# First-phase attention heads: operands written from PSUM into the attention's tiles, and the mLSTM's key units named first

## The chip, the cores and the metric

One core of a Trainium2 chip runs the kernel. The metric is device time in microseconds (us), of which smaller is better: a kernel is run several times and the median stands for it. A profile of one more execution shows every engine: TensorE (PE: matmuls, transposes), VectorE (DVE), ScalarE (ACT), GpSimd (POOL), SyncE (SP, which here issues nearly all DMA transfers).

## The reference

One layer of a hybrid encoder, run for 1024 frames of a new stream and 32 frames of a running one. The input is modulated, projected once, and the projection's columns go to three groups of heads: mLSTM (a matrix memory, 4 heads), FoX (attention with a forget gate, 8 heads of 64) and a gMLP gate. Their outputs are concatenated and projected, then a normalisation and a SwiGLU feed-forward follow. The attention part, cut:

```python
h = x * (1 + sc1) + sh1
mq, mk, mv, mo, mi, mf, fq, fk, fv, ff, gu, gv = jnp.split(h @ w_in, split_at, axis=-1)
...
def _fox_prompt(q, k, v, logf):
    Ft = jnp.cumsum(logf, axis=1).transpose(0, 2, 1)
...
        logits = (jnp.einsum('bthd,bshd->bhts', qi, k) * FOX_SCALE
                  + Fi[..., None] - Ft[:, :, None, :])
        logits = jnp.where(pos_k[None, :] <= pos_q[:, None], logits, -jnp.inf)
        p = jax.nn.softmax(logits, axis=-1)
        return jnp.einsum('bhts,bshd->bthd', p, v)
```

`fk` is also an output. The mLSTM needs the running sums and maxima of its gates (`li`, `lf`) before its chunks, and the forget gates of the attention come from the same small projection.

## The kernel before

All matmuls are in float32 precision by halves: each operand is split into a high half (rounded to the multiplier's format) and a low half (the rest), and a product is three matmuls (`gemm`, L112): hi x hi, hi x lo, lo x hi. The contraction over 1024 features is eight steps, so a block of 128 outputs by n frames costs 24 matmuls of n columns. Weights come in pieces of 512 KB (`raw`), ACT makes the high half (L105), DVE or POOL the low half (L106).

Frames come in two groups: group 0 is frames 0 to 511, group 1 the next 512 and the 32 of the running stream. A feature-major unit (`fm_unit`) projects 128 outputs; group 0 is cut into two pieces of 256 frames, group 1 into two of 272. Its results stand in a PSUM bank of pool "g", which has three.

For the attention a unit is one head: 64 rows of q and 64 of k. `evac_qk` (L359) takes a bank apart: ACT writes the scaled high half (`qkh`, L366), DVE the low half (`qkl`, L367), POOL their sum for the output k (`qkr`, L368). The halves are stored to the arrays `dqh` and `dql` in memory, the sum to the output. `fox` (L671) later loads a head's operands from there in eight loads and v in one: `qp` = (q hi over q lo), `k1` = (k hi twice), `q2` = (q hi, and four rows of the forget gates from `dfs`), `k2` = (k lo, and four such rows). Two matmuls per piece then give the logits S in a bank (L717 with `qp` and `k1`, L718 with `q2` and `k2`), DVE takes maxima, ACT the exponential (L726), PE transposes (L753), and so on to the output, which leaves its bank by an ACT copy (`fo`, L773) and a DVE addition (`fr`, L774).

In the first phase, `ORDER` (L42) names the units one after the other: q0 to q7 are the attention heads' projections, f0 to f7 their attention over the first 512 frames, k0 and k1 the mLSTM's keys (p: POOL makes the low halves), s the mLSTM's states, v and o token-major projections, m0 to m3 the mLSTM heads, a a piece of the late modulation (`ada`, L179 and following, which loads 512 KB into one of two buffers). The gates' code stands ahead of all of them. The text order isn't the order of execution: a list scheduler, which models the engines' times, places each engine's instructions; f and m units have high priority. Tiles come from pools with a fixed number of buffers per name, and an instruction that needs a buffer again waits for the buffer's last users. Each engine then takes its own instructions strictly in the placed order.

The attention's operand tiles stand in pool `mx0`, which is opened after the gates' pool is closed and uses its memory. The number of buffers is `foxbufs`: k1, qp and q2, k2, v, and one more.

Of the kernel before, what the change touches and what calls it, by code (L numbers as in the profile page):

```python
# [7 lines left out]
F32 = mybir.dt.float32  # L8
# [7 lines left out]
P = 128  # L16
D = 1024
KT = 8
# [20 lines left out]
MLB = (1, 2, 3, 4, 5)  # L39
RESE = "pp"  # L40
TAFF = ("aaaaaaaa", "aaaaaaav")
ORDER = "q0 f0 q1 a f1 a q2 f2 k0 k1p s a q3 f3 a v q4 f4 a q5 f5 o a m0 q6 f6 a m1 q7 m2 f7 a m3"  # L42
ADAPOS = 4
GENG = (0, 1, 1, 0)
FP = (0, 0)
# [20 lines left out]
def f(ap):  # L66
    return ap.bitcast(F32)


class Kernel:  # L70
# [10 lines left out]
    def t(self, pool, shape, dt=F32, tag=None, bufs=None):  # L81
        self.n += 1
        kw = {} if bufs is None else {"bufs": bufs}
        return pool.tile(shape, dt, tag=tag, name=f"{self.phase}_{tag}_{self.n}", **kw)
# [274 lines left out]
    def evac_qk(self, h):  # L359
        nc = self.nc  # L360

        def evac(o, n, ps):
            hi = self.t(self.sm, [P, 272], F32R, "qkh", 3)
            lo = self.t(self.sm, [P, 272], F32R, "qkl", 2)
            kr = self.t(self.sm, [P, 272], F32, "qkr", 3)
            nc.scalar.activation(hi[:, :n], ps, AF.Copy, scale=self.qsc)  # L366
            nc.vector.scalar_tensor_tensor(lo[:, :n], ps, self.qsc, f(hi[:, :n]), ALU.mult, ALU.subtract)  # L367
            nc.gpsimd.tensor_tensor(kr[:, :n], f(hi[:, :n]), f(lo[:, :n]), ALU.add)  # L368
            self.store(self.dqh[h, :, o:o + n], f(hi[:, :n]))
            self.store(self.dql[h, :, o:o + n], f(lo[:, :n]))  # L370
            self.store(self.d["o_kT"][h, :, o:o + n], kr[64:, :n])
            if o + n == T:
                nc.gpsimd.tensor_copy(self.qks[:, h, :], kr[:, n - NS:n])
        return evac

    def evac_mqk(self, i, scale):
        nc = self.nc

        def evac(o, n, ps):
            r = self.t(self.sm, [P, 272], F32, "qkr", 3)  # L380
            nc.scalar.activation(r[:, :n], ps, AF.Copy, scale=scale)
            self.store(self.dmqk[:, i, o:o + n], r[:, :n])
        return evac
# [288 lines left out]
    def fox(self, h, chunks):  # L672
        self.phase = "fox"
        mx = self.mx
        q0, q1 = chunks[0][0] * P, (chunks[-1][-1] + 1) * P
        nq, nk, nb = q1 - q0, q1, q1 // P
        t = lambda shape, dt, tag, bufs: self.t(mx, shape, dt, tag, bufs)
        b = self.foxbufs
        k1 = t([P, nk], F32R, "k1", b[0])
        qp = t([P, nq], F32R, "qp", b[1])  # L680
        k2 = t([68, nk], F32R, "k2", b[2])
        q2 = t([68, nq], F32R, "q2", b[1])
        v = t([P, nb, P], F32R, "v", b[3])
        qs = slice(q0, q1)
        self.load(f(qp[0:64]), self.dqh[h, 0:64, qs])
        self.load(f(qp[64:128]), self.dql[h, 0:64, qs])
        self.load(f(k1[0:64]), self.dqh[h, 64:128, :nk])
        self.load(f(k1[64:128]), self.dqh[h, 64:128, :nk])
        self.load(f(q2[0:64]), self.dqh[h, 0:64, qs])
        self.load(f(q2[64:68]), self.dfs[h, 2:6, qs])  # L690
        self.load(f(k2[0:64]), self.dql[h, 64:128, :nk])
        self.load(f(k2[64:68]), self.dfs[h, 0:4, :nk])
        self.load(f(v), self.dv[:, :nb, h * P:(h + 1) * P])
        for tiles in chunks:
            o = tiles[0] * P - q0
            n = len(tiles) * P
            yield from self.fox_chunk(h, tiles, nk, n, k1, k2, qp[:, o:o + n], q2[:, o:o + n], v)

    def fox_chunk(self, h, tiles, W, nq, k1, k2, qp, q2, v):
        nc, mx = self.nc, self.mx  # L700
        nb = tiles[-1] + 1
        t = lambda shape, dt, tag, bufs: self.t(mx, shape, dt, tag, bufs)
        b5 = self.foxbufs[4]
        probs = []
        for i in tiles:
            n = (i + 1) * P
            qc = slice((i - tiles[0]) * P, (i - tiles[0] + 1) * P)
            half = n if n <= 512 else (n // 2 + 127) // 128 * 128
            cuts = [(0, half)] + ([(half, n)] if half < n else [])
            mxs = self.t(mx, [P, 2], F32, "fmx", 3)  # L710
            sums = self.t(mx, [P, 2], F32, "fsm", 3)
            pr = t([P, W], F32, "p", 4)
            banks = []
            for x, (lo, hi) in enumerate(cuts):
                s = self.t(self.pss, [P, 512], F32, "s")
                w = hi - lo
                nc.tensor.matmul(s[:, :w], qp[:, qc], k1[:, lo:hi], start=True, stop=False)  # L717
                nc.tensor.matmul(s[:, :w], q2[:, qc], k2[:, lo:hi], start=False, stop=True)  # L718
                if hi == n:
                    nc.vector.tensor_tensor(s[:, w - P:w], s[:, w - P:w], self.maskneg, ALU.add)  # L720
                nc.vector.tensor_reduce(mxs[:, x:x + 1], s[:, :w], AX.X, ALU.max, negate=True)
                banks.append(s)
            if len(cuts) > 1:
                nc.vector.tensor_tensor(mxs[:, 0:1], mxs[:, 0:1], mxs[:, 1:2], ALU.min)  # L724
            for x, (lo, hi) in enumerate(cuts):
                nc.scalar.activation(pr[:, lo:hi], banks[x][:, :hi - lo], AF.Exp, bias=mxs[:, 0:1],  # L726
                                     accum_out=sums[:, x:x + 1])
            if len(cuts) > 1:
                nc.vector.tensor_tensor(sums[:, 0:1], sums[:, 0:1], sums[:, 1:2], ALU.add)
            nc.vector.reciprocal(sums[:, 0:1], sums[:, 0:1])  # L730
            if FP[tiles[0] // 4]:
                nc.scalar.activation(pr[:, :n], pr[:, :n], AF.Copy, scale=sums[:, 0:1])
            else:
                nc.vector.tensor_scalar(pr[:, :n], pr[:, :n], sums[:, 0:1], None, ALU.mult)
            probs.append(pr)
            yield
            self.phase = "fox"


        o = self.t(self.po, [P, 512], F32, "o")  # L740
        full = tiles[0] + 1
        order = [0] + list(range(full, nb)) + list(range(1, full))
        units = [order[x:x + 2] for x in range(0, nb, 2)] if full > 1 else [[0], [1], [2, 3]]
        held = None
        for unit in units:
            ps = self.t(self.pt, [P, 512], F32, "t")
            at, e = [], 0
            for b in unit:
                first = max(0, b - tiles[0])
                w = nq - first * P  # L750
                for y in range(first, len(tiles)):
                    c = e + (y - first) * P
                    nc.tensor.transpose(ps[:, c:c + P], probs[y][:, b * P:(b + 1) * P], self.ident)  # L753
                at.append((b, slice(e, e + w), slice(first * P, nq)))
                e += w
            ph = t([P, 512], F32R, "pth", b5)
            pl = t([P, 512], F32R, "ptl", 2)
            nc.scalar.copy(ph[:, :e], ps[:, :e])
            nc.vector.tensor_tensor(pl[:, :e], ps[:, :e], f(ph[:, :e]), ALU.subtract)
            for b, c, q in at:  # L760
                nc.tensor.matmul(o[:, q] if b == 0 else o[0:64, q], v[:, b, :] if b == 0 else v[:, b, 0:64],
                                 pl[:, c], start=b == 0, stop=False)
                if b == 0 and full == 1:
                    held = ph
                else:
                    nc.tensor.matmul(o[:, q], v[:, b, :], ph[:, c], start=False, stop=full > 1 and b == order[-1])
            yield
            self.phase = "fox"
        if held is not None:
            nc.tensor.matmul(o[:, :nq], v[:, 0, :], held[:, :nq], start=False, stop=True)  # L770
        tmp = t([64, nq], F32, "fo", 1)
        r = t([64, nq], F32, "fr", 1)
        nc.scalar.copy(tmp[:, :nq], o[64:128, :nq])  # L773
        nc.vector.tensor_tensor(r[:, :nq], o[0:64, :nq], tmp[:, :nq], ALU.add)  # L774
        c = tiles[0] // 4
        o = tiles[0] * P - GO[c]
        self.store(self.dmix[c][64 * (h % 2):64 * (h % 2) + 64, 2 + h // 2, o:o + nq], r[:, :nq])
# [474 lines left out]
    def run(self):  # L1252
# [68 lines left out]
        more(T1[3])  # L1321
        s2 = ExitStack()
        self.mx = self.pool("mx0", ctx=s2)
        self.foxbufs = (2, 1, 1, 2, 3)

        def emit(x):
            eng = nc.gpsimd if x[-1] == "p" else nc.vector
# [4 lines left out]
            if x[0] == "m":  # L1332
                return self.mlstm(i)
            if x[0] == "q":
                self.fm_unit(w3[2 + i], self.evac_qk(i), (0, 1) if i < QD else (0,), eng)
            elif x[0] == "k":
                self.fm_unit(w3[i], self.evac_mqk(2 + i, 0.125), eng=eng)
            elif x[0] == "s":
# [256 lines left out]
```

## Time and profile before

| | us |
|---|---|
| median of the three runs | 1391.1 (1388.4 to 1398.72) |
| profiled execution, its own time | 1389.64 |
| its span in the trace | 1387.8 |

The tables of the profile are read like this. A timeline row has the start in us, the duration, the engine, the line, the operation, the output and the inputs by the program's names, the shape and the count; in brackets the idle time before it and what ended it. A row of the waits' table has the engine and line, what was waited for, the total in us, how often, and the longest. A row of the windows' table has the stretch, its length, each engine's busy time with its instruction count (PE, its weight loads, DVE, ACT, POOL), the granted PE clock, the DMA share and GB/s. A group's row has the count, the busy time in us and the mean in ns, then the idle time before it and what ended it.

### The profile page before, as it was taken

What the parts mean: (1) busy time and instruction counts of PE and PEld (TensorE: products, weight loads), DVE (VectorE), ACT (ScalarE), POOL (GpSimd) and SP (SyncE); (2) the same over time, 40 slices, a digit from 0 to 9 for tenths busy, and PEclk for the clock granted to TensorE, in tenths of its full rate; (3) what the DMA queues carried; (4) which work ended last, traced back from release to release, by engine and by line L of the source; (5) the groups of instructions that cost most, each with busy time, mean ns of one, the idle gap of its engine ahead of it and who ended that gap; (6) DMA issues with size and microseconds to landing.
All of it is one profiled execution on the core that took longest, in us unless ns stands there. A gap on an engine that the chain in (4) does not pass through costs nothing.

```text
span 1387.8 us, 25846 instructions
## 1 busy us (share of the span) xinstructions
PE 1344.1 (97%) x9651; PEld 1236.2 (89%) x9651; DVE 1030.4 (74%) x2190; ACT 641.0 (46%) x1249; POOL 260.2 (19%) x292
## 2 busy tenths in 40 slices
PE   7999999999999799999999999999999999999996
PEld 4899988899999678888887889899999999999996
DVE  5548656678788657777776766678898988888777
ACT  3313234444555344545544455345574544545355
POOL 0103200052267400000000000264610000000341
PEclk9999999999999899999999999999999999999998
DMA  9764577585765665554543442564587767453321
GB/s 361 260 217 135 165 239 213 173 252 167 234 209 152 194 182 155 141 140 118 138 117 86 112 122 81 192 176 132 159 221 200 217 163 205 145 176 113 102 90 65
DMA packets 133557, 233.09 MB, mean 168 GB/s; under 512 B 22308, under 2 KB 75180, under 8 KB 133432
## 3 DMA queue, kind: packets, MB, share of 16 engines
q1 hardware_dynamic: 128120, 221.34, 51.7%
q0 software_dynamic: 5168, 9.96, 4.7%
q8 instruction: 76, 1.25, 0.4%
q14 instruction: 49, 0.40, 0.1%
q10 hardware_dynamic: 144, 0.14, 0.0%
HBM read 197.50 MB, written 53.81 MB: 181 GB/s over the span
## 4 chain that ended last, share of the span: by engine, by line
PE 69%; DVE 4%; DMA 2%; ACT 1%; issue 1%; POOL 0%; SPq 0%; DVEq 0%; ACTq 0%
PE up_g L117 5%; PE up_g L118 5%; PE up_g L119 5%; PE dn_g L119 4%; PE dn_g L117 4%; PE dn_g L118 4%; PE sup_u L119 3%; PE sup_u L117 3%; PE sup_u L118 3%; PE wo_g L118 2%; PE wo_g L119 2%; PE wo_g L117 2%; PE sup_g L118 2%; PE sup_g L119 2%; PE sup_g L117 2%; PE fox_t L753 2%
## 5 line engine op out<-in xcount | busy, mean ns | idle before, releaser
L117 PE MATMUL up_g<-mlstm_ah,up_whi 128*128 128x512 f32 (+1 forms) x384 | 142.8, 372 | 3.6 <-DVE fm_qkl L367 2.7
L118 PE MATMUL up_g<-mlstm_al,up_whi 128*128 128x512 f32 (+1 forms) x384 | 143.0, 372 | 0.6 <-DVE mlstm_al L1008 0.6
L119 PE MATMUL up_g<-mlstm_ah,up_wlo 128*128 128x512 f32 (+1 forms) x384 | 142.4, 371 | 0.0
L284 PE MATMUL tm_g<-tm_whi,start_h1l 128*128 128x256 f32 (+1 forms) x384 | 110.0, 287 | 0.0
L282 PE MATMUL tm_g<-tm_whi,start_h1h 128*128 128x256 f32 (+1 forms) x384 | 109.6, 287 | 0.0
L283 PE MATMUL tm_g<-tm_wlo,start_h1h 128*128 128x256 f32 (+1 forms) x384 | 109.5, 286 | 0.0
L117 PE MATMUL fm_g<-start_h1h,fm_whi 128*128 128x256 f32 (+2 forms) x344 | 102.1, 302 | 6.9 <-DVE fm_qkl L367 2.7
L118 PE MATMUL fm_g<-start_h1l,fm_whi 128*128 128x256 f32 (+2 forms) x344 | 101.5, 295 | 0.2 <-DVE start_h1l L223 0.2
L119 PE MATMUL fm_g<-start_h1h,fm_wlo 128*128 128x256 f32 (+2 forms) x344 | 100.6, 294 | 0.0
L1127 ACT CAST sup_whi<-sup_raw 128x1024 fp32r<-128x1024 f32 x54 | 56.0, 1048 | 90.3 <-PE dn_u L118 46.5
L117 PEld LDWEIGHTS up_g<-mlstm_ah,up_whi 128*128 128x128 f32 x384 | 74.5, 194 | 16.2 <-DVE fm_qkl L367 2.9
L118 PEld LDWEIGHTS up_g<-mlstm_al,up_whi 128*128 128x128 f32 x384 | 74.6, 194 | 12.6 <-DVE up_actl L1061 0.8
L119 PEld LDWEIGHTS up_g<-mlstm_ah,up_wlo 128*128 128x128 f32 x384 | 74.6, 194 | 10.7
L105 ACT CAST up_whi<-up_raw 128x1024 fp32r<-128x1024 f32 x50 | 52.4, 1049 | 61.1 <-PE dn_g L118 22.5
L726 ACT ACTIVATE fox_p<-fox_s,fox_fmx 128x384 f32<-128x384 f32 (+2 forms) x96 | 55.1, 579 | 49.1 <-DVE fox_fmx L724 43.6
L117 PEld LDWEIGHTS fm_g<-start_h1h,fm_whi 128*128 128x128 f32 x344 | 65.3, 191 | 12.7 <-DVE fm_qkl L367 3.2
L982 DVE SCALAR_TENSOR_TENSOR wo_z<-dn_g,start_mod,wo_z 128x512 f32<-128x512 f32 (+4 forms) x120 | 60.3, 521 | 21.1 <-PE dn_g L119 20.5
L1128 DVE TENSOR_TENSOR sup_wlo<-sup_raw,sup_whi 128x1024 fp32r<-128x1024 f32 x54 | 68.0, 1263 | 10.4 <-ACT sup_whi L1127 10.4
L282 PEld LDWEIGHTS tm_g<-tm_whi,start_h1h 128*128 128x128 f32 x384 | 72.3, 189 | 1.9 <-issue 1.2
L284 PEld LDWEIGHTS tm_g<-tm_whi,start_h1l 128*128 128x128 f32 x384 | 72.3, 188 | 1.5 <-issue 1.2
L117 PE MATMUL dn_g<-up_acth,dn_whi 128*128 128x512 f32 (+2 forms) x200 | 73.5, 368 | 0.0
L118 PE MATMUL dn_g<-up_actl,dn_whi 128*128 128x512 f32 (+2 forms) x200 | 73.4, 368 | 0.0
(571 smaller groups left out, 4591.4 us busy)
## 6 DMA issues: line engine op xcount, KB each, us to landing
up_raw<-w_gu SPq DMA_DIRECT2D x50, 512.0 KB
dn_raw<-w_dn SPq DMA_DIRECT2D x28, 512.0 KB
ada_late<-w_ada SPq DMA_DIRECT2D x24, 512.0 KB
wo_raw<-w_o SPq DMA_DIRECT2D x24, 512.0 KB
sup_raw<-w_gu SPq DMA_DIRECT2D x20, 512.0 KB
start_dp<-w_gu SPq DMA_DIRECT2D x19, 512.0 KB
start_dp<-w_gu POOLq DMA_DIRECT2D x19, 512.0 KB, 7.7
sup_raw<-start_dp SPq DMA_DIRECT2D x18, 512.0 KB
```

Of the source, the lines that this page charges most:

```text
L105: nc.scalar.copy(hi[:, :w], raw[:, :w])
L117: nc.tensor.matmul(ps, hi, xh(k), start=start and k == 0, stop=False)
L118: nc.tensor.matmul(ps, hi, xl(k), start=False, stop=False)
L119: nc.tensor.matmul(ps, lo, xh(k), start=False, stop=stop and k == n - 1)
L282: nc.tensor.matmul(ps[:, :ncol], xh, hi, start=k == 0, stop=False)
L283: nc.tensor.matmul(ps[:, :ncol], xh, lo, start=False, stop=False)
L284: nc.tensor.matmul(ps[:, :ncol], xl, hi, start=False, stop=k == 7)
L726: nc.scalar.activation(pr[:, lo:hi], banks[x][:, :hi - lo], AF.Exp, bias=mxs[:, 0:1], accum_out=sums[:, x:x + 1])
L753: nc.tensor.transpose(ps[:, c:c + P], probs[y][:, b * P:(b + 1) * P], self.ident)
L982: self.lastz = self.nc.vector.scalar_tensor_tensor(z[:, m, x:y], ps[:, x - a:y - a], g[i], z[:, m, x:y], ALU.mult, ALU.add)
L1127: nc.scalar.copy(h, x)
L1128: tt(l, x, f(h), ALU.subtract)
```

## The change

1. `ORDER` names k0 and k1p first, then q0 f0 q1, and s stands before q2.
2. A q unit is no longer an `fm_unit` but a `head_unit`. It makes one product of 512 columns for group 0, in one bank, and writes the halves from that bank into the attention's tiles: ACT writes q hi into `qp`, DVE q lo beside it, ACT k hi into one half of `k1`, DVE k lo into `k2`, ACT k hi again into the other half of `k1` and q hi into `q2`; two ACT copies take k for the output. Only the halves of k go to `dqh` and `dql`. The four forget-gate rows of `q2` and `k2`, and v, are still loaded. Heads 0 and 1 project their group 1 as before.
3. `fox` takes a head's tiles where `head_unit` left them; the second phase loads them as before.
4. `foxbufs` is (2, 2, 2, 2, 3) for (2, 1, 1, 2, 3); `qkh` and `qkr` have two buffers for three.
5. The output's `fo` and `fr` are one tile.

```diff
-ORDER = "q0 f0 q1 a f1 a q2 f2 k0 k1p s a q3 f3 a v q4 f4 a q5 f5 o a m0 q6 f6 a m1 q7 m2 f7 a m3"
+ORDER = "k0 k1p q0 f0 q1 a f1 s a q2 f2 a q3 f3 a v q4 f4 a q5 f5 o a m0 q6 f6 a m1 q7 m2 f7 a m3"
...
-            hi = self.t(self.sm, [P, 272], F32R, "qkh", 3)
+            hi = self.t(self.sm, [P, 272], F32R, "qkh", 2)
             lo = self.t(self.sm, [P, 272], F32R, "qkl", 2)
-            kr = self.t(self.sm, [P, 272], F32, "qkr", 3)
+            kr = self.t(self.sm, [P, 272], F32, "qkr", 2)
...
+    def head_tiles(self, h, nq, nk):
+        b = self.foxbufs
+        t = lambda shape, tag, bufs: self.t(self.mx, shape, F32R, tag, bufs)
+        return (t([P, nk], "k1", b[0]), t([68, nk], "k2", b[2]), t([P, nq], "qp", b[1]), t([68, nq], "q2", b[1]),
+                t([P, nk // P, P], "v", b[3]))
+
+    def head_unit(self, h):
+
+        nc = self.nc
+        w = self.weights(self.d["w_in_f"][2 + h], KT, P)
+        self.phase = "head"
+        k1, k2, qp, q2, v = self.heads[h] = self.head_tiles(h, 512, 512)
+        self.load(f(q2[64:68]), self.dfs[h, 2:6, :512])
+        self.load(f(k2[64:68]), self.dfs[h, 0:4, :512])
+        self.load(f(v), self.dv[:, :4, h * P:(h + 1) * P])
+        ps = self.t(self.pg, [P, 512], F32, "g")
+        self.gemm(ps, w, slice(0, P), *self.h1parts(0, 512))
+        lo, hi = slice(0, 64), slice(64, 128)
+        nc.scalar.activation(qp[lo], ps[lo], AF.Copy, scale=0.125)
+        nc.vector.scalar_tensor_tensor(qp[hi], ps[lo], 0.125, f(qp[lo]), ALU.mult, ALU.subtract)
+        nc.scalar.copy(k1[hi], ps[hi])
+        nc.vector.tensor_tensor(k2[lo], ps[hi], f(k1[hi]), ALU.subtract)
+        nc.scalar.copy(k1[lo], ps[hi])
+        nc.scalar.activation(q2[lo], ps[lo], AF.Copy, scale=0.125)
+        for o in (0, 256):
+            kr = self.t(self.sm, [P, 272], F32, "qkr", 2)
+            nc.scalar.copy(kr[hi, :256], ps[hi, o:o + 256])
+            self.store(self.d["o_kT"][h, :, o:o + 256], kr[hi, :256])
+        self.store(self.dqh[h, hi, :512], f(k1[hi]))
+        self.store(self.dql[h, hi, :512], f(k2[lo]))
+        if h < QD:
+            evac = self.evac_qk(h)
+            self.phase = "fm"
+            for o, n in self.ranges((1,)):
+                ps = self.t(self.pg, [P, 512], F32, "g")
+                self.gemm(ps[:, :n], w, slice(0, P), *self.h1parts(o, n))
+                evac(o, n, ps[:, :n])
...
-            r = self.t(self.sm, [P, 272], F32, "qkr", 3)
+            r = self.t(self.sm, [P, 272], F32, "qkr", 2)
...
+        if h in self.heads:
+            k1, k2, qp, q2, v = self.heads.pop(h)
+        else:
+            k1, k2, qp, q2, v = self.head_tiles(h, nq, nk)
...
-        tmp = t([64, nq], F32, "fo", 1)
-        r = t([64, nq], F32, "fr", 1)
-        nc.scalar.copy(tmp[:, :nq], o[64:128, :nq])
-        nc.vector.tensor_tensor(r[:, :nq], o[0:64, :nq], tmp[:, :nq], ALU.add)
+        r = t([64, nq], F32, "fo", 1)
+        nc.scalar.copy(r[:, :nq], o[64:128, :nq])
+        nc.vector.tensor_tensor(r[:, :nq], o[0:64, :nq], r[:, :nq], ALU.add)
...
-        self.foxbufs = (2, 1, 1, 2, 3)
+        self.foxbufs = (2, 2, 2, 2, 3)
+        self.heads = {}
...
-                self.fm_unit(w3[2 + i], self.evac_qk(i), (0, 1) if i < QD else (0,), eng)
+                self.head_unit(i)
```

More of the change, by code (lines that the diff above doesn't have):

```diff
@@ L676, in fox @@
         nq, nk, nb = q1 - q0, q1, q1 // P
[L677 to L693, printed above, removed]
+        if h in self.heads:
+            k1, k2, qp, q2, v = self.heads.pop(h)
+        else:
+            k1, k2, qp, q2, v = self.head_tiles(h, nq, nk)
+            qs = slice(q0, q1)
+            self.load(f(qp[0:64]), self.dqh[h, 0:64, qs])
+            self.load(f(qp[64:128]), self.dql[h, 0:64, qs])
+            self.load(f(k1[0:64]), self.dqh[h, 64:128, :nk])
+            self.load(f(k1[64:128]), self.dqh[h, 64:128, :nk])
+            self.load(f(q2[0:64]), self.dqh[h, 0:64, qs])
+            self.load(f(q2[64:68]), self.dfs[h, 2:6, qs])
+            self.load(f(k2[0:64]), self.dql[h, 64:128, :nk])
+            self.load(f(k2[64:68]), self.dfs[h, 0:4, :nk])
+            self.load(f(v), self.dv[:, :nb, h * P:(h + 1) * P])
         for tiles in chunks:
```

## The prediction, made before the changed kernel was run

> **What bounds the kernel now.** I read the page's busy table and chain of waits first, then the table of waits of TensorE (PE), then the timeline at those waits, and last the windows around them.
>
> ```profile
> PE 1344.1 (97%) x9651; PEld 1236.2 (89%) x9651; DVE 1030.4 (74%) x2190; ACT 641.0 (46%) x1249; POOL 260.2 (19%) x292
> PE 69%; DVE 4%; DMA 2%; ACT 1%; issue 1%; POOL 0%; SPq 0%; DVEq 0%; ACTq 0%
> ```
>
> PE is the bound: 97% busy. ScalarE (ACT) and GpSimd (POOL) have room. A change can pay only by shortening PE's matmuls or by closing holes in PE's line. These are the holes in the part that changes:
>
> ```profile
> PE fox_s L717 <- DMA fox_qp<-start_dql: 4.3, 3, 1.7
> PE fm_g L117 <- DVE fm_qkl L367: 2.7, 1, 2.7
> ```
>
> ```profile
> 137.33 0.28 PE L119 MATMUL fm_g<-start_h1h,fm_wlo 128*128 128x256 f32 x1
> ...
> 138.04 0.28 PE L119 MATMUL fm_g<-start_h1h,fm_wlo 128*128 128x256 f32 x1
> 141.02 0.58 PE L117 MATMUL fm_g<-start_h1h,fm_whi 128*128 128x256 f32 x1 [2.70 <-DVE fm_qkl L367]
> ```
>
> ```profile
> 105.00:170.00 65.00, 62.30 (x512) 61.36 (x511) 49.32 (x120) 19.09 (x41) 19.45 (x29) 0.97 0.49 143
> 170.00:215.00 45.00, 43.27 (x348) 37.50 (x347) 24.00 (x74) 17.10 (x47) 1.46 (x2) 1.00 0.80 241
> 215.00:260.00 45.00, 42.34 (x354) 39.26 (x352) 25.59 (x65) 20.07 (x51) 3.68 (x5) 1.00 0.73 212
> ```
>
> At 141 us PE waits 2.70 us for an evacuation (fm_qkl) that stands on VectorE (DVE) in the middle of the mLSTM gates; behind it a matmul takes 0.58 us instead of 0.28, and the window's granted clock is 0.97: 3% of 65 us, so about 2.0 us more. That hole costs 4.7 us. The other three are the loads of the attention's operands:
>
> ```profile
> 202.66 0.47 PE L717 MATMUL fox_s<-fox_k,fox_qp 128*128 128x128 f32 x2 [1.73 <-DMA fox_qp<-start_dql]
> 218.20 0.47 PE L717 MATMUL fox_s<-fox_k,fox_qp 128*128 128x128 f32 x2 [1.34 <-DMA fox_qp<-start_dql]
> 255.71 0.47 PE L717 MATMUL fox_s<-fox_k,fox_qp 128*128 128x128 f32 x2 [1.20 <-DMA fox_qp<-start_dql]
> ```
>
> These are 4.27 us, and the clock of their windows stays at 1.00, so no more hangs on them.
>
> **The loads removed.** Per head the stores and reloads of qp, k1, k2 and q2 go, so the three waits above have nothing left to wait for: minus 4.3 us. What takes the load's place is a chain on ACT and DVE that reads the PSUM bank; for heads 1 to 7 the order has 40 or more PE rows (at 0.118 us, 4.7 us) between the end of a head's product and the head's first S row, so I count no new wait there in the likeliest case. SyncE (SP) issues 56 instructions fewer; the small rows of the forget gate (4 partitions of q2 and k2) and v are still loaded, long before their use.
>
> **The wider product.** A head's product is 24 matmuls of 512 columns in place of 48 of 256.
>
> ```profile
> 801.48 0.39 PE L119 MATMUL dn_g<-up_acth,dn_wlo 128*128 128x512 f32 x1
> ...
> 802.88 0.39 PE L119 MATMUL dn_g<-up_acth,dn_wlo 128*128 128x512 f32 x1
> ```
>
> Six matmuls lie between the starts in both pairs: 1.40/6 = 0.233 us for 512 columns, 0.71/6 = 0.118 us for 256. So 24 x 0.233 = 5.60 against 48 x 0.118 = 5.68: 0.08 a head, minus 0.6 us for eight. For 272 columns I scale: 0.118 x 272/256 = 0.126.
>
> **The new start of the attention.** This is the term that decides. On PE, around head 0's first S products, before (names: fm_g is a projection's PSUM bank, tm_g a token-major one, fox_s the S bank, ada_t a late modulation row):
>
> ```order
> L118 MATMUL fm_g_2511<-start_h1l_170,fm_whi_2507 128x256
> L717 MATMUL fox_s_1703<-fox_k_282_1686,fox_qp_1687 128x128
> L717 MATMUL fox_s_1714<-fox_k_282_1686,fox_qp_1687 128x256
> L119 MATMUL fm_g_2511<-start_h1h_169,fm_wlo_2508 128x256
> L117 MATMUL fm_g_2511<-start_h1h_169,fm_whi_2507 128x256
> ```
>
> and now (gates_t are the gates' transposes):
>
> ```order
> L117 MATMUL fm_g_2036<-start_h1h_171,fox_whi_1985 128x272
> L118 MATMUL fm_g_2036<-start_h1l_172,fox_whi_1985 128x272
> L119 MATMUL fm_g_2036<-start_h1h_171,fox_wlo_1986 128x272
> L185 MATMUL ada_t_1496<-start_ident_121,ada_adas_1509 128x128 x2
> L179 MATMUL ada_t_1518<-ada_late_1519,start_c_63_182 32x256 x4
> L752 MATMUL fox_s_1904<-head_k_288_1785,head_qp_1787 128x128
> L752 MATMUL fox_s_1915<-head_k_288_1785,head_qp_1787 128x256
> L753 MATMUL fox_s_1904<-head_k_289_1786,head_q_291_1788 128x128
> L753 MATMUL fox_s_1915<-head_k_289_1786,head_q_291_1788 128x256
> ```
>
> The S rows moved from PE's row 1061 to its row 928, right behind the gates, with no projection left to fill ahead of them. What they need hangs on ACT. Before, ACT's rows around the decay factor d0c (an exponential of two small rows that the gates send out and fetch back through memory):
>
> ```order
> L381 ACTIVATE fm_qkr_2413<-fm_g_2388 128x256
> L513 ACTIVATE fm_d0c_2480<-fm_d0c_2480 128x18
> L381 ACTIVATE fm_qkr_2441<-fm_g_2416 128x272
> L495 ACTIVATE start_col_178<-start_col_178 128x9x12
> L182 COPY ada_adas_1509<-ada_t_1496 128x256
> ```
>
> and now:
>
> ```order
> L366 ACTIVATE fm_qkh_1891<-fm_g_1866,start_qsc_147 128x272
> L551 ACTIVATE fox_d0c_2216<-fox_d0c_2216 128x18
> L394 ACTIVATE head_qp_1787<-head_g_1793 64x512
> L394 ACTIVATE head_qp_1991<-head_g_1997 64x512
> L533 ACTIVATE start_col_178<-start_col_178 128x9x12
> L182 COPY ada_adas_1509<-ada_t_1496 128x256
> L396 COPY head_k_288_1785<-head_g_1793 64x512
> L396 COPY head_k_334_1989<-head_g_1997 64x512
> L398 COPY head_k_288_1785<-head_g_1793 64x512
> L399 ACTIVATE head_q_291_1788<-head_g_1793 64x512
> ```
>
> The first head's evacuation now stands behind d0c, and ACT takes its rows in order. Their times, with the gates' last steps on DVE, and then the forms of 64x512 and 64x256:
>
> ```profile
> 163.79 0.22 ACT L513 ACTIVATE fm_d0c<-fm_d0c 128x18 f32<-128x18 f32 x1 [3.27 <-DMA fm_d0c<-start_dd]
> ...
> 164.43 0.28 ACT L495 ACTIVATE start_col<-start_col 128x108 f32<-128x108 f32 x1
> 165.12 0.37 ACT L182 COPY ada_adas<-ada_t 128x256 f32<-128x256 f32 x1 [0.40 <-PE ada_t L179]
> ```
>
> ```profile
> 134.33 0.28 DVE L439 TENSOR_TENSOR gates_fr<-gates_ft,gates_fr 8x128 fp32r<-8x128 f32 x1 [0.87 <-ACT gates_fr L438]
> ...
> 136.62 2.47 DVE L440 TENSOR_SCALAR gates_fr<-gates_fr 8x256 fp32r<-8x256 f32 x1
> ...
> 141.00 0.28 DVE L440 TENSOR_SCALAR gates_fr<-gates_fr 8x256 fp32r<-8x256 f32 x1
> ...
> 144.02 1.11 DVE L440 TENSOR_SCALAR gates_fr<-gates_fr 8x256 fp32r<-8x256 f32 x1
> ...
> 146.97 0.47 DVE L367 SCALAR_TENSOR_TENSOR fm_qkl<-fm_g,start_qsc,fm_qkh 128x256 fp32r<-128x256 f32 x1
> ...
> 156.40 0.15 DVE L479 TENSOR_TENSOR gates_d<-gates_m0x,gates_me 4x9 f32<-4x9 f32 x1
> 156.58 1.35 DVE L487 TENSOR_TENSOR gates_rs<-gates_rb,gates_me 4x1152 f32<-4x1152 f32 x1
> ```
>
> ```profile
> L773 ACT COPY fox_fo<-fox_o 64x256 f32<-64x256 f32 x16 | 5.9, 370 | 15.0 <-PE fox_o L766 14.8
> L773 ACT COPY fox_fo<-fox_o 64x512 f32<-64x512 f32 x8 | 4.7, 584 | 3.7 <-PE fox_o L770 3.6
> L774 DVE TENSOR_TENSOR fox_fr<-fox_o,fox_fo 64x512 f32<-64x512 f32 x8 | 5.4, 677 | 0.8 <-ACT fox_fo L773 0.8
> ```
>
> Call T the end of gates_rs, 157.9 before. On DVE the order has six evacuations (fm_qkl) between the gates' steps before, and one now:
>
> ```order
> L505 COPY gates_me_1433<-gates_cm_243_1417 4x1
> L506 TENSOR_TENSOR gates_m_244_1432<-gates_me_1433,gates_gb_1414 4x1
> L367 TENSOR_SCALAR fm_qkl_1858<-fm_g_1832,start_qsc_147,fm_qkh_1857 128x272
> L504 TENSOR_SCALAR gates_cm_243_1417<-gates_cm_242_1416,gates_m_244_1432 4x128
> L505 COPY gates_me_1433<-gates_cm_243_1417 4x1
> ```
>
> That is where this one moved: PE's second head product waits for it. Five fewer are 5 x 0.47 = 2.4 us. If the stretched steps shrink to 0.28 too, as POOL loses its work beside them, another 2.2 + 0.8 go, and the 0.87 that DVE waited for ACT. T then lies between 157.9 - 2.4 = 155.5 and 157.9 - 6.3 = 151.6; below this I allow 149, as more rows like these may shrink. I take 152, near the end where the stretch goes with its cause.
>
> d0c started 163.79 - 156.55 = 7.2 us after gates_d ended and 5.9 after T; its loads and stores are unchanged, so it ends at T + 6.1. Then ACT does two qp (2 x 0.58), col 0.28, adas 0.37 and the first k1 0.58: T + 8.5. DVE's k2 (0.68) and ACT's second k1 (0.58) follow one on the other: S can start at T + 9.7 = 161.7.
>
> PE reached row 873 at 138.2, so row 801, up to which the widths are the same, at 138.2 - 72 x 0.118 = 129.7. The first head's product (5.6) and two of 272 (6.0) end at 141.3. From there to S it has the second head's product 5.6, one of 272 at 3.0, twelve late modulation rows and eleven transposes at no more than 0.12 (2.8): 11.4. It loses 161.7 - 141.3 - 11.4 = **9.0 us** (6 for T = 149, 12.5 for 155.5) in two or three waits: for fm_qkl_1858, for the evacuation behind gates_rs, and for adas and S. A halved clock inside this stretch is hidden by it; the last wait, some 4 us, can leave 2.0 us of it behind: 0 to 2, I take 1. The next product waits for the bank that q2 (0.58) and two copies of 0.37 still read, less four S rows: 0.7.
>
> One price stands outside: ada_t_1518's load of 512 KB starts only when ada_t_1496 has read the buffer, some 6 us before S. Its nearest row is on another queue:
>
> ```profile
> start_dp<-w_gu POOLq DMA_DIRECT2D x19, 512.0 KB, 7.7
> ```
>
> At 7.7 it ends last by 1.7 us; I take 0, since this stretch moves little else (DMA share 0.49 above), and keep 1.7 for the range.
>
> [...]
>
> **Later stretches.** ACT gets four operations of 0.58 and two of 0.37 a head (3.1) for two of 0.47 (0.9): 17 us more in all, in windows where it is busy 17 to 20 us of 45. DVE gets 2 x 0.68 for 2 x 0.48, POOL gives up two additions. Beside PE this is free where work lies between. Not free is the copy of k: only two buffers are left, and an exponential stands behind a copy that waits for a store. A store's wait was seen here:
>
> ```profile
> L381 ACT ACTIVATE fm_qkr<-fm_g 128x256 f32<-128x256 f32 x4 | 1.5, 385 | 10.1 <-DMA o_kT<-fm_qkr 4.5 <-PE fm_g L119 2.5 <-issue 1.7
> ```
>
> 4.5 us over four; a head product of 5.6 us stands on PE behind the first of these, so I take 1 us, between 0 and 4.5. After about 385 us PE's order is the same as before. The merged fo/fr tile and the two extra operand buffers need no instruction.
>
> **Sum.** 9.0 + 1 + 0.7 + 1 = 11.7 added; 4.7 + 4.3 + 0.6 = 9.6 removed: +2.1. The profiled execution took 1389.6 us (span 1387.8, 1.8 around it), 1.5 under the median of the three runs. 1389.6 + 2.1 = **1392 us**. Its bounds: -9.6 + 6 + 0.7 = -2.9, so 1387, to -9.6 + 12.5 + 2 + 0.7 + 1.7 + 4.5 = +11.8, of which I keep 10, since not all are bad at once: 1399.
>
> **Rivals.**
> *A, the holes only change places:* the new waits cost what the wait at 141 did (4.7), since d0c is fetched sooner with fewer stores queued ahead on SP. For it: 56 instructions go from that queue. Against it: DMA was not busy there. 1389.6 - 4.3 - 0.6 = 1385.
>
> *B, slower:* the ACT queue at the k copies. Two buffers, and each next copy waits for a store, with the exponentials behind it. It decides from the point where PE has under 4.5 us (38 rows at 0.118) between an exponential and the transposes that read it. At four heads of eight that is 4 x 4.5 = 18 us: 1410. For it: ACT takes its rows strictly in order and gets the copies in place of POOL. Against it: ACT is half idle, and the order puts head products there.
>
> *C, wide matmuls gain more:* if a 512-column matmul followed at the pace of a 256-column one, 24 x 0.118 would go from each of eight heads: 22.7 us, 1392 - 22 = 1370. The row of 0.233 speaks against it. [...]
>
> *D, not what it says:* the S rows still wait for a load, the small rows or v, as long as they did for qp: the 4.3 stay, 1396. Against it: they are issued early.
>
> **The numbers.** Forecast 0.50, A 0.18, B 0.14, C 0.02, D 0.10, and 0.06 for what I don't see, half to each side. Two runs of this kernel can't be told apart under about 1% (14 us). Faster by that: C and half the unseen, 0.05. Slower: B, less a little where it strikes fewer heads, and half the unseen, 0.15. Within: 0.80. The forecast's own range is 1387 to 1399; with A below and smaller forms of B above, 1381 to 1404 leaves out about 2 in 10.
>
> **What would show it.** No wait of fox_s for fox_qp; d0c's exponential ending about 6 us after gates_rs, with the first qp behind it; S's first row near 162; a wait of 3 to 5 us right ahead of it; pace 0.233 in the head products. It would be wrong if S starts under 8 us after gates_rs, if T stays at 157, or if the waits after 170 us grow rather than go.

## The result and the profile after

| | median, us | ratio to before (95% interval) |
|---|---|---|
| before, 20 runs | 1390.06 | |
| changed kernel, 20 runs | 1386.86 | 0.9972 [0.9961, 0.9982] |
| changed kernel again on another chip (11 runs; before 1387.49) | 1385.75 | 0.9977 [0.9961, 0.9993] |

The change makes the kernel 3.2 us faster by the medians where 2.1 us slower had been forecast. (The ratios and their intervals are estimated from all runs; the quotients of the medians are 0.9977 and 0.9987.) First the same views as before. The waits of TensorE (PE) in the changed kernel:

```profile
PE up_g L117 <- ACT lna_tmp L1037: 3.4, 1, 3.4
PE ada_t L179 <- DMA ada_late<-w_ada: 2.8, 1, 2.8
PE fm_g L117 <- DVE fm_qkl L367: 2.4, 2, 2.0
PE mlstm_t L598 <- DVE fox_ptl L794: 2.2, 1, 2.2
...
PE fox_s L752 <- ACT fox_p L761: 1.9, 1, 1.9
```

No wait of fox_s for a load is left, and the wait of 2.7 us at 141 us is gone. New are the wait for a late modulation's load and one of the mLSTM's transposes behind the attention. Its windows:

```profile
105.00:170.00 65.00, 61.66 (x446) 56.51 (x445) 47.52 (x131) 22.56 (x50) 12.76 (x20) 0.95 0.40 121
170.00:215.00 45.00, 44.91 (x328) 38.40 (x327) 32.00 (x88) 26.01 (x67) 2.12 (x3) 1.00 0.65 199
215.00:260.00 45.00, 45.00 (x331) 40.00 (x330) 22.49 (x55) 22.52 (x52) 1.13 (x2) 1.00 0.49 158
```

From 170 to 260 us the busy time of PE shows hardly a hole (89.9 of 90 us, before 85.6). From 105 to 170 us it lost more than before: 61.66 us busy for 62.30, at a clock of 0.95 for 0.97.

The start of the attention, in the timelines of DVE, ACT and PE:

```profile
149.92 1.35 DVE L525 TENSOR_TENSOR gates_rs<-gates_rb,gates_me 4x1152 f32<-4x1152 f32 x1
```

```profile
156.05 0.22 ACT L551 ACTIVATE fox_d0c<-fox_d0c 128x18 f32<-128x18 f32 x1 [8.51 <-DMA fox_d0c<-start_dd]
156.17 1.05 ACT L394 ACTIVATE head_qp<-head_g 64x512 fp32r<-64x512 f32 x2
...
159.19 0.58 ACT L398 CAST head_k<-head_g 64x512 fp32r<-64x512 f32 x1 [0.44 <-DVE head_k L397]
```

```profile
157.72 0.44 PE L185 MATMUL ada_t<-start_ident,ada_adas 128*128 128x128 f32 x2 [0.15 <-ACT ada_adas L182]
160.97 1.08 PE L179 MATMUL ada_t<-ada_late,start_c 128*32 128x256 f32 x8 [2.81 <-DMA ada_late<-w_ada]
161.98 0.80 PE L752 MATMUL fox_s<-head_k,head_qp 128*128 128x128 f32 x2
```

The gates end at T = 151.3 (152 was taken), and S starts at 162.0 (161.7). But the reason is another one: the evacuation is done at 159.8, T + 8.5, and PE stands for 2.8 us before the load of 512 KB. That load was the price put at 0, with 1.7 us kept for the range.

### The profile page after: what moved, and what is told of

The parts are those of the page before. It is cut to its first block, busy times and chain, and to the rows that moved or that the text cites. A ratio compares the mean times of both kernels' runs of the same rounds, so it can differ in the third digit from the quotient of the medians.

```text
span 1384.6 us, 25402 instructions
## 1 busy us (share of the span) xinstructions
PE 1343.1 (97%) x9459; PEld 1226.1 (89%) x9459; DVE 1031.2 (74%) x2190; ACT 655.5 (47%) x1281; POOL 244.8 (18%) x276
## 4 chain that ended last, share of the span: by engine, by line
PE 83%; DVE 9%; DMA 4%; ACT 2%; issue 2%; POOL 1%; SPq 0%; DVEq 0%; ACTq 0%; POOLq 0%
PE up_g L117 5%; PE up_g L118 5%; PE up_g L119 5%; PE dn_g L119 4%; PE dn_g L117 4%; PE dn_g L118 4%; PE tm_g L282 3%; PE tm_g L283 3%; PE tm_g L284 3%; PE sup_u L119 3%; PE sup_u L117 3%; PE sup_u L118 3%; PE wo_g L118 2%; PE wo_g L119 2%; PE wo_g L117 2%; PE fox_t L788 2%
## 5 line engine op out<-in xcount | busy, mean ns | idle before, releaser
L119 PEld LDWEIGHTS up_g<-mlstm_ah,up_wlo 128*128 128x128 f32 x384 | 73.2, 191 | 10.6
L106 DVE TENSOR_TENSOR up_wlo<-up_raw,up_whi 128x1024 fp32r<-128x1024 f32 x50 | 66.8, 1336 | 14.0 <-ACT up_whi L105 13.3
L283 PEld LDWEIGHTS tm_g<-tm_wlo,start_h1h 128*128 128x128 f32 x384 | 72.3, 188 | 2.3 <-issue 2.1
L119 PE MATMUL dn_g<-up_acth,dn_wlo 128*128 128x512 f32 (+2 forms) x200 | 73.3, 366 | 0.0
L117 PE MATMUL fm_g<-start_h1h,fm_whi 128*128 128x272 f32 (+2 forms) x200 | 60.6, 312 | 5.9 <-DVE fm_qkl L367 2.0
```

The source lines that it names most:

```text
L106: (eng or nc.vector).tensor_tensor(lo[:, :w], raw[:, :w], f(hi[:, :w]), ALU.subtract)
L117: nc.tensor.matmul(ps, hi, xh(k), start=start and k == 0, stop=False)
L119: nc.tensor.matmul(ps, lo, xh(k), start=False, stop=stop and k == n - 1)
L283: nc.tensor.matmul(ps[:, :ncol], xh, lo, start=False, stop=False)
```

## The experiments

Single executions of one kernel differ by several us (28 runs of the kernel before on one chip lie between 1383.8 and 1392.1), so three profiles of each kernel were compared by stage (the repeated profiles below supply the others). For every matmul I took the time to the next matmul's start, less the usual distance for its width (the median over the run); the sum over a stage is PE's loss there. The part of it that falls on half clock (stretches in which the granted clock is 0.50) comes from the granted clock in windows of 1 us. Means of three profiles, us:

| stage, us | before: waits + half clock | after: waits + half clock | difference |
|---|---|---|---|
| 0 to 105 (unchanged) | 20.1 + 0 | 20.3 + 0 | +0.2 |
| 105 to 170, gates, start of attention | 3.8 + 1.7 | 5.5 + 3.4 | +3.4 |
| 170 to 260, heads 0 to 3 | 15.3 + 0.6 | 8.3 + 0 | -7.6 |
| 260 to 345, mLSTM and heads | 8.5 + 0 | 10.6 + 0 | +2.1 |
| 345 to 400 | 4.9 + 0 | 5.9 + 2.3 | +3.3 |
| 400 to 480, order unchanged | 10.8 + 5.4 | 9.9 + 2.3 | -4.0 |
| 480 to 1365, order unchanged | 29.6 + 2.0 | 28.3 + 1.7 | -1.6 |

The sum is -4.2; with the 0.6 us of the wider product it is -4.8, and the mean spans (1388.5 and 1383.8) differ by 4.7. The half clock is 9.7 us in all in both: it moved, and as a whole it neither gave nor took. The timed runs agree: on the second chip their granted clock is 0.991 on the mean, before and after. The 4.7 us are more than the 3.2 of the medians, and two of the three profiles of before took 2.8 and 4.0 us more than the median of their chip (1389.35 for 1386.53, 1392.09 for 1388.12).

Where the difference is made shows at the first row from which PE's order is the same to the end in both kernels (6677 matmuls), first before, then after:

```profile
386.19 0.28 PE L118 MATMUL wo_g<-mlstm_al,wo_whi 128*128 128x256 f32 x1
```

```profile
389.39 0.47 PE L118 MATMUL wo_g<-mlstm_al,wo_whi 128*128 128x256 f32 x1
```

In the other profiles it starts at 389.5 and 390.7 us before, at 389.9 and 389.6 after. The changed kernel thus comes there no sooner, 0.8 us later on the mean. What is left takes 1001.6, 998.1 and 999.5 us before and 995.2, 994.0 and 993.3 after. By the table, waits fell by 2.2 us and half clock rose by 3.4 between 105 and 400 us; behind 400 us waits fell by 2.2 and half clock by 3.4. So in these profiles what the removed loads give is given back inside the changed part, and the difference lies behind it, in instructions that the change leaves as they were.

**The two parts of the change, each alone.** The new ORDER in the kernel before:

```diff
-ORDER = "q0 f0 q1 a f1 a q2 f2 k0 k1p s a q3 f3 ..."
+ORDER = "k0 k1p q0 f0 q1 a f1 s a q2 f2 a q3 f3 ..."
```

> The kernel before with the new ORDER alone (keys first), operands still through memory. If the gain is the removed loads: no gain here, 0 to +3 us, since the loads' waits (4.3 us) stay. If the gain comes from the gates ending earlier with no evacuations between them: -2 to -4 us, and the wait of 2.7 us at 138 us is gone.

Measured: 1.0006 [0.9990, 1.0022]. The two waits as its waits' table has them:

```profile
PE fox_s L717 <- DMA fox_qp<-start_dql: 3.4, 2, 2.1
PE gates_t L492 <- DVE gates_rs L487: 2.0, 1, 2.0
```

The order alone gives nothing: the loads' waits stay, and the wait for an evacuation among the gates is replaced by one of 2.0 us for the gates themselves. The other half, the changed kernel with the old ORDER:

> The changed kernel with the old ORDER: operands straight from PSUM, keys after head 2. If the gain is the removed loads: -3 to -5 us; the first S no longer stands behind the decay factor, so the stall of 3 us ahead of it should be smaller. If the order is what pays: 0 to +2 us.

Measured: 1412.84 us against 1386.53, 1.0194 [1.0169, 1.0219], 26 us slower. Both expectations fall. Its timeline of PE, its waits and the window:

```profile
130.87 0.29 PE L119 MATMUL fm_g<-start_h1h,fox_wlo 128*128 128x272 f32 x1
154.73 2.15 PE L530 MATMUL gates_t<-start_ident,gates_rs 128*128 128x128 f32 x9 [23.57 <-DVE gates_rs L525]
```

```profile
154.61 1.07 ACT L394 ACTIVATE head_qp<-head_g 64x512 fp32r<-64x512 f32 x2 [14.11 <-DVE gates_rs L525]
```

```profile
105.00:170.00 65.00, 37.56 (x231) 31.83 (x230) 43.20 (x126) 16.19 (x38) 7.69 (x18) 0.74 0.29 83
```

PE stands still for 23.6 us until the gates end. The heads' first evacuation (head_qp) waits for the same instruction, since the operand tiles lie in the gates' memory, so the two heads' banks, two of three, stay full (ACT then empties both, x2). The third is full as well: the product of 272 columns that ends before the wait is copied out only at 167.8 us, because its copy needs a buffer that POOL frees late, after the first head's stores of k.

```profile
167.00 1.48 POOL L368 TENSOR_TENSOR fm_qkr<-fm_qkh,fm_qkl 128x272 f32<-128x272 f32 x2 [21.41 <-DMA o_kT<-head_qkr]
```

```profile
167.79 0.49 ACT L366 ACTIVATE fm_qkh<-fm_g,start_qsc 128x272 fp32r<-128x272 f32 x1 [2.65 <-POOL fm_qkr L368]
```

The two buffers of qkh and qkr may thus have a share in this stall; the old ORDER with three was not run. With loads, the heads' products were emptied at once into buffers of their own and went to memory; PE could run on. The key units are then the cover. To test that, one of them was moved back:

```diff
-ORDER = "k0 k1p q0 f0 q1 a f1 s a q2 f2 ..."
+ORDER = "k0 q0 f0 q1 a f1 k1p s a q2 f2 ..."
```

> The changed kernel with only k0 ahead of the heads and k1p behind f1. If the two key units are the cover while two heads' banks stay held until the gates end: one unit is 96 matmuls of about 0.122 us, 11.7 us of cover less than with both, so PE waits 12 us for gates_rs and the time is 8 to 13 us over the changed kernel. If the 24 us of the old ORDER come from something else (the scheduler's other choices): no such relation, under 3 us over or as much as 24.

Measured: 1405.24 us, 1.0122 [1.0102, 1.0143], some 19 us over the changed kernel on that chip (1385.75), more than the 8 to 13 expected, and

```profile
PE gates_t L530 <- DVE gates_rs L525: 11.0, 1, 11.0
```

The wait is 23.6 us with no key unit ahead, 11.0 with one, and with two it is gone: one covers 12.6 us (its 96 matmuls of about 0.122 us make 11.7), and the other the 11.0 that are left. So the wait came as the first case has it and the time did not: of the 19 us, 14 are lost from 105 to 170 us (22.8 for the changed kernel's 8.9), and the rest later, which was not followed up.

**Is it the single buffer or the round trip?** The kernel before with the changed buffers alone:

```diff
-        self.foxbufs = (2, 1, 1, 2, 3)
+        self.foxbufs = (2, 2, 2, 2, 3)
```

with qkh and qkr at two and the merged fo tile, as in the change.

> The kernel before with two buffers for k2, qp and q2, two for qkh and qkr, and the merged output tile; operands still loaded. If the load waits of 4.3 us come from the single buffer of qp (the next head's load can't start before the last S of this one): those waits go and the time falls by 3 to 5 us without any head unit. If they come from the round trip through memory: waits of 1 us or more stay, -1 to +1 us.

Measured: 1.0002 [0.9985, 1.0019], and its waits are

```profile
PE fox_s L717 <- DMA fox_q<-start_dfs: 2.2, 1, 2.2
...
PE fox_s L717 <- DMA fox_qp<-start_dql: 1.0, 1, 1.0
```

The loads still come last, partly under another name, and the time is unchanged: the round trip was the cause, not the single buffer. Two buffers for qkh and qkr alone:

> The kernel before with two buffers for qkh and qkr in place of three, nothing else. Theory B (fewer buffers alter how the stores of the last heads' second group line up behind 430 us): the wait for fm_qkl ahead of the first up product falls from 2.5 to under 1 us and the time by 1 to 3 us. Theory A: no change, or 1 to 3 us slower in the first phase, since each buffer waits longer for its stores.

Measured: 1.0011 [0.9998, 1.0024]. The wait ahead of the first up product fell to 0.7 us as theory B had it, but the time did not fall: the next wait there (lna_tmp) is 3.7 us, where the three profiles of before have 0.6, 3.4 and 1.9. The kernel with the order alone shows the same pair, 0.7 and 3.6, with three buffers, so the buffers need not be the cause.

**Repeated profiles.**

> The kernel before, profiled once more, to see how much two profiles of one kernel differ. Theory A (the gain of 3.2 us is made in the first phase, up to 385 us): the wait of the up product at 452 us (2.7 us), the one of ada_g at 469 us (4.1 us) and the one at 743 us (2.9 us) come back within 0.5 us each, and the matmuls behind 105 us start within 0.5 us of the first profile. Theory B (those later waits move by chance from one execution to the next): one of them differs by more than 1 us.

> A third profile of the kernel before. If the half clock behind 400 us belongs to this kernel: again 5 to 7 us lost to it between 450 and 480 us. If it moves by chance: under 3.5 us. The loss of the stages without the half clock should be as in the first two within 1 us each: 4 us in 105 to 170, 15 in 170 to 260, 8.4 in 260 to 345.

> The changed kernel, profiled and timed once more. Theory A (the gain is the removed loads, given back in part by the wait ahead of S): the holes of 170 to 260 us stay gone, 5 to 7 us less lost there than before; the wait ahead of S for the late modulation's load is again 2.5 to 3.5 us; the median is 3 to 4 us under that of before. Theory B (the gain stands behind 400 us): the hole ahead of the first up product is under 1 us again, against 2.3 to 2.7 us in both profiles of before.

> A third profile of the changed kernel. If the half clock keeps its places: 3.4 us at 160, 1.7 at 371, 1.7 at 467 us. Without the half clock again 5.6 us lost in 105 to 170, 8.3 in 170 to 260, 10.5 in 260 to 345.

The second profile of before has the wait at 469 us at 2.0 instead of 4.1 and that at 743 at 1.3 instead of 2.9: they move, theory B of that run. The third lost 4.9 us to the half clock between 400 and 480 us, between its two cases, and without it 3.6, 15.6 and 8.9 in the three stages asked for. The changed kernel's second profile has 2.9 us ahead of S for the load and no wait over 0.9 ahead of the first up product, so the signs of both its theories came and it does not decide between them; the third 2.9 us again, 3.4 us of half clock in each of the three stages named, where 3.4, 1.7 and 1.7 were expected, and 5.3, 8.4 and 10.7 in the stages. So the stages' waits repeat within about 2 us, and the half clock between 400 and 480 us is 4.5 to 6.8 us before and 1.7 to 3.4 after. The windows of 450 to 480 us show it, first before, then after:

```profile
450.00:480.00 30.00, 22.09 (x140) 19.74 (x139) 19.28 (x45) 10.80 (x27) 14.45 (x21) 0.77 0.68 184
```

```profile
450.00:480.00 30.00, 23.57 (x176) 21.67 (x175) 24.35 (x56) 16.21 (x38) 18.02 (x25) 0.94 0.72 185
```

**The wait ahead of S.** The second late modulation unit was moved behind f1:

```diff
-T1 = (1, 1, 0, 2)
+T1 = (1, 1, 0, 1)
-ORDER = "k0 k1p q0 f0 q1 a f1 s a q2 ..."
+ORDER = "k0 k1p q0 f0 q1 a f1 a s a q2 ..."
```

> The changed kernel with the second late modulation unit behind f1 in place of ahead of the heads. If the load of 512 KB is what S waited for: that wait of 2.8 us goes, S starts 1.5 to 2.2 us sooner (the evacuation chain ended 2.2 us before S), and the time is 1 to 2 us under the changed kernel. If the stall ahead of S costs nothing (its time is given back by a later wait): no change within 0.5 us.

Measured: 1384.39 us, 0.9971 [0.9957, 0.9985], 1.4 us under the changed kernel's 1385.75 on the same chip, which is inside the intervals, so the times do not decide between the two cases. In the profile S starts at 160.1 us for 162.0. The load's wait is gone, and the evacuation is what S waits for now:

```profile
PE fox_s L752 <- ACT head_k L398: 1.7, 1, 1.7
```

So the wait for the load was 1.1 us longer than the one for the evacuation chain that takes its place. The half clock behind it stayed at 3.4 us.

Then PE was given work ahead of S: the unit v, named later before, stands in front of the heads.

```diff
-ORDER = "k0 k1p q0 f0 q1 a f1 s a q2 f2 a q3 f3 a v q4 ..."
+ORDER = "k0 k1p v q0 f0 q1 a f1 s a q2 f2 a q3 f3 a q4 ..."
```

> The changed kernel with the token-major unit v ahead of the heads, so that PE has some 25 us more work between the keys and the first S. If PE merely reaches the first S too early: the waits ahead of S (0.5 + 0.3 + 3.0 + 0.5 us) and the two half-clock stretches behind them (3.4 us) go, 5 to 7 us, and the time is 3 to 6 us under the changed kernel. If that work is missed later as cover: the waits of the mLSTM and attention behind 300 us (2.4 and 2 to 3 us) grow by as much and the time stays within 1.5 us.

Measured: 1379.19 us against 1388.12, **0.9936 [0.9913, 0.9958]**: faster than both kernels, as the first case expected (the one run of the changed kernel on this chip took 1384.94, its medians on the other chips are 1386.86 and 1385.75). Its window and the first S:

```profile
105.00:170.00 65.00, 65.00 (x534) 61.82 (x532) 42.17 (x117) 18.59 (x43) 11.05 (x17) 1.00 0.45 134
```

```profile
172.87 0.29 PE L119 MATMUL fm_g<-start_h1h,tm_wlo 128*128 128x272 f32 x1
173.00 0.39 PE L752 MATMUL fox_s<-head_k,head_qp 128*128 128x128 f32 x2
```

PE is busy for all of the 65 us at full clock, and S follows without a hole: 2.7 us lost in this stage for 8.9. Behind it the stages lose about what they did (8.0, 12.7, 7.3 and 12.4 us).

> Both moves at once: v ahead of the heads and the second late modulation unit behind f1. With v as cover that load no longer stands in the way, so the second move should add nothing: within 1 us of the kernel with v alone. If the load still stops PE there: 1 to 2 us under it.

Measured: 1386.48 us, 0.9981 [0.9964, 0.9998]. Both expectations miss: it is 7 us over the kernel with v alone. Its runs lie between 1380.4 and 1389.4, and the profile is of one near the upper end (1388.34). The stage ahead of S is as good (1.6 us lost), but a new wait stands at 377 us:

```profile
PE wo_g L117 <- DVE fm_qkl L367: 5.6, 1, 5.6
```

The scheduler placed the later units otherwise; why this evacuation comes so late was not followed up.

## Why the prediction was wrong

The bound, the loads' waits as what the heads give, and the place of the new wait were right. Two steps of the sum failed where it mattered for the sign: the arrival of PE at the new start, reckoned too early, and the rest of the kernel, put at 0. Up to 400 us the measured terms come to +0.6 us (3.4 - 7.6 + 5.4 - 0.6) where +2.1 was forecast. That these lie close is luck, as three of the four are off by 2.6 to 4.4 us. With the -5.6 behind 400 us and the +0.2 ahead of 105 they make the -4.8 of the profiles. The signs of being wrong that the prediction names all look at the changed part, and none of them came.

**The new start, +6.0 forecast (9.0 + 1 + 0.7 less the 4.7 at 141 us), +3.4 measured.** The failed step is "PE reached row 873 at 138.2". The wait at 141 us stands ahead of a product of 256 columns, but of that at row 849. The timeline of before has the row at which the products of 256 columns (order row 801) begin:

```profile
132.45 0.28 PE L117 MATMUL fm_g<-start_h1h,fm_whi 128*128 128x256 f32 x1
```

From there to the wait are 5.7 us, 48 matmuls, where the step had reckoned 72. PE therefore came 24 x 0.118 = 2.8 us later to the second head's product, and what was left to wait shrinks as much, 9.0 to 6.2; with that alone the sum is -0.7, on the other side of zero. In the profile the losses between the gates and S add to 4.6 us (0.5 + 0.3 + 3.0 + 0.3 + 0.5), as that execution was also 1.8 us later at 105 us, and PE found no wait at all for fm_qkl_1858. The DVE steps that T rests on shrank as estimated: the two of 2.47 and 1.11 us (L440) are gone, and the eight of this form take 0.28 to 0.30 us (L478). That POOL's work beside them had stretched them is not shown: before, POOL is busy for all of the 2.47 and the 1.11 us, but in the changed kernel it is busy for 0.23 us of a step that takes 0.29 (at 134.27). That S itself came when forecast is luck: d0c ended at T + 5.0 rather than T + 6.1, T was 151.3 and not 152, and the load put at 0 was what came last. The half clock took 3.4 us, not 0 to 2.

**The loads, -4.3 forecast, -7.6 measured.** The right mechanism from too few rows: one profile's three named waits. In the other profiles of before a fourth S waits too: 2.0 us at 241 us in the second, where the profile names no load, and 1.0 us for a load of k at 244 us in the third. Of the 7.6, 0.6 are half clock, and the small losses under the table's notice went too; which of these hang on the loads was not separated. SyncE issues 64 instructions fewer, not 56.

**Later in the first phase, +1 forecast between 0 and 4.5, +5.4 measured (260 to 400 us).** It isn't the k copies on ACT: none of the sixteen (head_qkr, L402) has idle time ahead of it. It is the mLSTM's transposes behind the attention (2.2 to 2.5 us) and an evacuation at 369 us (2.0 to 3.0, where before another one cost 1.1 to 1.4), with 2.3 us of half clock. That these come from work used up earlier as cover is an argument, not shown; with v moved ahead they stayed as they were.

**Behind 400 us, 0 forecast, -5.6 measured.** The step is "After about 385 us PE's order is the same as before". The order is the same, but the time is not. The half clock there fell by 3.4 us on the mean. It is not shown that the change does this: it costs 8.5, 5.1 and 8.5 us in the profiles of before and 3.4, 3.4 and 5.1 in those of after, but 5.1 with the order alone, 1.7 with the buffers alone and 8.5 in the changed kernel with the late modulation moved. The rest, 2.2 us over almost 1000 us, is about as much as profiles of one kernel differ. The wait ahead of the first up product fell by 2 us in all three, but it did so too with the order alone and with two buffers for qkh and qkr alone, which are not faster. So how much of the 3.2 us is made here, and by what, stays open.

The wider product is as reckoned:

```profile
138.12 0.40 PE L118 MATMUL head_g<-start_h1l,fm_whi 128*128 128x512 f32 x1
...
139.52 0.40 PE L118 MATMUL head_g<-start_h1l,fm_whi 128*128 128x512 f32 x1
```

Six matmuls in 1.40 us are 0.233 each, so rival C is out. Rival B (ACT and the copies of k) did not come, nor did D. Rival A, 1385 us, came nearest in number, though not by its mechanism: d0c was indeed fetched 1 us sooner, but the new start costs 3.4 us more than the hole that it replaced.

What the prediction missed altogether is what ORDER is for. It weighed the order only by the S rows that it brings forward. The runs show that the heads' direct evacuation costs 26 us without it, and that it gives nothing by itself; the gain of 0.28% is that of the pair. Where in the kernel the pair makes it, three profiles do not settle.

## What to carry to other kernels

Writing results straight from PSUM into operand tiles saves a round trip (whose waits were 4.3 us in the first profile of before), but it ties the bank to the moment at which those tiles come free. Where they share memory with an earlier stage, as here, the heads' banks stay full until that stage ends, and PE needs other work in front for just as long (it stood for 23.6 us with no key unit ahead, for 11.0 with one): count it in matmuls, and put it there in the program's order. When a time of arrival is worked out by counting rows back from a wait, check against the trace which row that wait belongs to; 24 matmuls, 2.8 us, were more here than the whole sum forecast (2.1). And when a gain of 0.3% is explained by profiles, compare the time at which the unchanged part begins: here it begins no sooner.

## What the runs showed of the hardware that was not expected

In these profiles the half clock (granted clock 0.50) came in stretches of 3.4 or 6.8 us, which cost 1.7 or 3.4 us each, long standstills and the end of the run aside. In one of them, in the changed kernel, matmuls of 272 columns start 0.227 us apart (163.00 to 165.95 us); at full clock it is 0.125 (153.22 to 155.34 us). With the late modulation moved, PE stood for 1.8 us ahead of S and then ran at half clock for 6.8 us:

```profile
158.00:161.00 3.00, 1.21 (x6) 0.77 (x6) 2.40 (x7) 2.51 (x6) 0.00 (x0) 0.91 0.41 92
161.00:164.00 3.00, 3.00 (x13) 2.83 (x13) 2.05 (x8) 2.28 (x8) 0.24 (x1) 0.50 0.74 207
164.00:167.00 3.00, 3.00 (x15) 3.00 (x15) 0.50 (x1) 0.51 (x2) 1.48 (x3) 0.50 0.86 240
```

Elsewhere a wait of 1.73 us (at 202.7 us, before) left the clock at 1.00. Why half clock followed the one and not the other is not shown.
